# The delta rule's triangular inverse on 32x32 diagonal squares instead of whole 128x128 tiles

## Chip, core and metric

The kernel runs on one core of one Trainium2 chip. The metric is device time in microseconds (us), the median over runs; lower is better. One further execution was profiled, and its trace is what the views below are taken from.

## What is computed

Two layers of a hybrid trunk (a gated delta rule beside band attention, then a Mamba-2 mixer, each followed by a squared-ReLU MLP) on 256 positions of width 2048, all in f32. The edit touches one place of the first layer, the gated delta rule, with 8 heads of width 128. In the reference it works on chunks of 64 positions:

```python
lower = jnp.where(strict, jnp.einsum('bhnid,bhnjd->bhnij', kb, kc) * decay, 0.0)
eye = jnp.eye(CHUNK, dtype=f32)
tmat = lax.linalg.triangular_solve(eye + lower, jnp.broadcast_to(eye, lower.shape),
                                   left_side=True, lower=True, unit_diagonal=True)
u = jnp.einsum('bhnij,bhnje->bhnie', tmat, vc * bc[..., None])
w = jnp.einsum('bhnij,bhnjd->bhnid', tmat, kb * jnp.exp(gcum)[..., None])
```

`tmat` is the inverse of a unit lower triangular matrix. It then goes into every product with the values and the state. The kernel takes chunks of 128 positions, so it inverts a 128x128 matrix for each head and each of two chunks.

## The kernel before

The kernel is written for a scheduler: the Python code emits instructions through generators, and the framework places them on the five engines, in an order fixed at build time; on each engine instructions run in that order. The main thread emits weight blocks one after the other: a DMA brings 1 MB of weights (`raw`), ScalarE casts a half of them (`wh`, line 332), VectorE forms the rest (`wl`, line 336), and TensorE multiplies (line 322, the tiles `pg` and `pw`). After every few products a tick lets a step of the background generators in; each `yield` in such a generator ends a step. VectorE besides works off a stream of modulation rows, the `mraw` products of line 456.

The delta rule is such a background task, `gdn_group`, once for each of two head groups of four heads (`hg` 0 and 1); the second begins when the first is done. A group has two tiles, `gdn_tile` with `t` = 0 and 1, of 128 positions each, and steps them in turn. In a tile, `lt` (`gLt`) is the transposed strict lower triangle of four heads, 128x512, and the inverse is built by doubling: `x` (`gX`) holds the inverse of the diagonal blocks of size s, `xt` (`gXt`) its transpose. A level s takes, for each head, a product of `lt` and `x`, a mask and copy by VectorE into `y` (`gY`, cleared by GpSimd before), a product of `xt` and `y`, a subtraction by VectorE, and a transpose of `x` by TensorE that ScalarE copies into `xt`:

```python
for s in (2, 4, 8, 16, 32, 64):
    ...
    for h in range(4):
        self.mm(ps[:, h], lt[:, h], x[:, h])
    ...
    nc.vector.tensor_tensor(part(y, 0), part(ps, 0), self.M[s].unsqueeze(1).to_broadcast([P, 4, nb, s]), op=ALU.mult)
```

Level 64 makes the last update on `xt` itself and needs no transpose. The products `mm` (line 325) and transposes `tr` (line 329) of f32 tiles go to PSUM tiles `pm`, of which four buffers rotate. Beside the inverse the same stretch holds the attention of the same heads (`att_group`, score products `pm<-u,u`, transposes with `anti` and `aT`). When both tiles have an `x`, `gdn_group` sets the flag `prep`, which lets the attention of the first group start.

The masks of the levels (`lev2` to `lev64`, `lev1T`) are made by GpSimd at the start, in `masks`.

Of the kernel before, what the change touches and what calls it, by code (L numbers as in the profile page):

```python
# [12 lines left out]
I32 = mybir.dt.int32  # L13
AF = mybir.ActivationFunctionType
ALU = mybir.AluOpType
# [3 lines left out]
P = 128  # L19
# [93 lines left out]
class Trunk:  # L113
# [287 lines left out]
    def masks(self):  # L401
        nc = self.nc
        g = nc.gpsimd

        self.U = self.const([P, P], "Umask")
        g.memset(self.U, 1.0)
        g.affine_select(out=self.U, in_=self.U, compare_op=ALU.is_ge, fill=0.0, base=0, pattern=[[1, P]], channel_multiplier=-1)
        self.SU = self.const([P, P], "SUmask")
        g.memset(self.SU, 1.0)
        g.affine_select(out=self.SU, in_=self.SU, compare_op=ALU.is_ge, fill=0.0, base=-1, pattern=[[-1, P]], channel_multiplier=1)  # L410

        self.Uc = self.const([P, P], "Ucmask")
        g.tensor_copy(self.Uc, self.U)
        g.tensor_scalar(self.Uc[:64], self.Uc[:64], -1.0, None, op0=ALU.add)
        self.anti = self.const([P, P], "anti")
        g.memset(self.anti, 1.0)
        g.affine_select(out=self.anti, in_=self.anti, compare_op=ALU.is_equal, fill=0.0, base=1 - P, pattern=[[1, P]], channel_multiplier=1)

        self.M = {}
        for s in (2, 4, 8, 16, 32, 64):  # L420
            nb = P // (2 * s)
            m = self.const([P, nb, s], f"lev{s}")
            g.memset(m, 1.0)
            g.affine_select(out=m, in_=m, compare_op=ALU.is_ge, fill=0.0, base=-s, pattern=[[-2 * s, nb], [0, s]], channel_multiplier=1)
            g.affine_select(out=m, in_=m, compare_op=ALU.is_ge, fill=0.0, base=2 * s - 1, pattern=[[2 * s, nb], [0, s]], channel_multiplier=-1)
            self.M[s] = m

        self.M1T = self.const([P, 64, 2], "lev1T")
        g.memset(self.M1T, 0.0)
        v = self.M1T[:, :, 1:2]  # L430
        g.memset(v, 1.0)
        g.affine_select(out=v, in_=v, compare_op=ALU.is_equal, fill=0.0, base=0, pattern=[[-2, 64], [0, 1]], channel_multiplier=1)
        self.M1T = self.M1T.rearrange("p b c -> p (b c)")


    def mod_start(self, layer):
# [610 lines left out]
    def gdn_tile(self, hg, t, kf, qf, vf, G):  # L1047

        nc = self.nc
        H = slice(hg * 4, hg * 4 + 4)
        T = slice(t * P, t * P + P)
        v = self.small(8, "gss")
        for n, src in ((0, kf), (1, qf)):
            ps = self.pm()
            for h in range(4):
                self.tr(ps[:, h], src[:, h, T])
            if n == 0 and t == 0:
                kd = self.s2(tag="gkd")  # L1060
# [24 lines left out]
        nc.scalar.activation(E, ps, AF.Exp)  # L1085
        nc.vector.tensor_tensor(E, E, self.row(self.U), op=ALU.mult)
        yield
        ps = self.pm()
        for h in range(4):
            self.tr(ps[:, h], vf[:, h, T])  # L1090
        V = self.s2(tag="gV")
        nc.vector.tensor_tensor(V, ps, self.bc(nk), op=ALU.mult)
        G["V", t] = V
        yield

        ps = self.pm()
        for h in range(4):
            self.mm(ps[:, h], kf[:, h, T], kf[:, h, T])
        lt = self.s2(tag="gLt")
        for h in range(4):  # L1100
            nc.vector.scalar_tensor_tensor(lt[:, h], ps[:, h], be[:, h : h + 1], E[:, h], op0=ALU.mult, op1=ALU.mult)

        xt = self.s2(tag="gXt")
        nc.vector.tensor_tensor(xt, lt, self.row(self.M1T), op=ALU.mult)
        nc.vector.tensor_tensor(xt, self.row(self.ident), xt, op=ALU.subtract)
# [8 lines left out]
        ps = self.pm()  # L1114
        for h in range(4):
            self.tr(ps[:, h], xt[:, h])
        x = self.s2(tag="gX")
        nc.scalar.copy(x, ps)
        G["X" + str(t)] = x
        yield  # L1120


        for s in (2, 4, 8, 16, 32, 64):
            nb = P // (2 * s)
            part = lambda a, n: a.rearrange("p h (b n c) -> p h b n c", n=2, c=s)[:, :, :, n]
            ps = self.pm()
            for h in range(4):
                self.mm(ps[:, h], lt[:, h], x[:, h])
            y = self.s2(tag="gY")
            nc.gpsimd.memset(y, 0.0)  # L1130
            nc.vector.tensor_tensor(part(y, 0), part(ps, 0), self.M[s].unsqueeze(1).to_broadcast([P, 4, nb, s]), op=ALU.mult)
            yield
            ps = self.pm()
            if s < 64:
                for h in range(4):
                    self.mm(ps[:, h], xt[:, h], y[:, h])
                nc.vector.tensor_tensor(part(x, 0), part(x, 0), part(ps, 0), op=ALU.subtract)
                yield
                ps = self.pm()
                for h in range(4):  # L1140
                    self.tr(ps[:, h], x[:, h])
                nc.scalar.copy(xt, ps)
            else:
                for h in range(4):
                    self.mm(ps[:, h], y[:, h], xt[:, h])
                nc.vector.tensor_tensor(part(xt, 1), part(xt, 1), part(ps, 1), op=ALU.subtract)
                yield
        G["Xt", t] = xt

    def gdn_group(self, hg, kc, qc, vc, gates):  # L1150

        nc = self.nc
# [3 lines left out]
        G = {}  # L1156
        tiles = [Task(self.gdn_tile(hg, t, kf, qf, vf, G)) for t in range(2)]
        while not all(t.done for t in tiles):
            for t in tiles:
                if not t.done:  # L1160
                    t.step()
            if all("X" + str(n) in G for n in range(2)):
                self.prep[hg].done = True
            yield

        ps = self.pm()
        for h in range(4):
# [4 lines left out]
        ps = self.pm()  # L1172
# [5 lines left out]
        ps = self.pm()  # L1178
# [11 lines left out]
        ps = self.pm()  # L1190
# [6 lines left out]
        for t in range(2):  # L1197
            yield
            ps = self.pm()
# [24 lines left out]
        for t in range(2):  # L1224
            ps = self.pm()
# [608 lines left out]
```

## Time and profile before

| | |
|---|---|
| median of 3 runs | 2707.59 us (2705.99 to 2708.86) |
| the profiled execution | 2705.89 us, span 2704.0 us |
| TensorE's granted clock | 0.993 of full speed |
| HBM read | 675.33 MB |

The span is the time from the first to the last instruction of the profiled execution. "Busy" is the time in which an engine had at least one instruction under way. Matmuls overlap: one of 0.275 us can be followed by the next after 0.11 us, so the time that a row of them takes on TensorE is read from where the next begins. PE is TensorE's multiplication, PEld its loading of weights, DVE is VectorE, ACT ScalarE, POOL GpSimd. Rows of a timeline give start, length, engine, line, operation, the tiles written and read, and a count. Rows of groups give a count, then busy time and the mean of one in ns, then the idle time before them. Rows of a tile give the least, median and greatest duration in ns.

### The profile page before, as it was taken

To read this page: it belongs to the slowest core of one execution; us is meant where nothing else is said; L and a number is where in the kernel's file an instruction comes from. 1 tells how busy PE (TensorE), PEld (TensorE's weight loads), DVE (VectorE), ACT (ScalarE), POOL (GpSimd) and SP (SyncE) were. 2 spreads that over 40 slices of the span, in tenths; PEclk is the share of its full clock that TensorE was granted. 3 is DMA by queue.
4 is the path that set the end of the run, shared out by engine and by line. 5 is a ranking of instruction groups with operands and counts; after the bars stand their busy time and mean duration, and the time that the engine had idled before them with its cause. 6 is when DMAs were issued, how large, how long until landed. Compare 5 with 4: busy or idle time off the path is not lost.

```text
span 2704.0 us, 39515 instructions
## 1 busy us (share of the span) xinstructions
PE 2646.9 (98%) x15578; PEld 2337.1 (86%) x15578; DVE 2155.6 (80%) x3106; ACT 1348.6 (50%) x1990; POOL 24.2 (1%) x98
## 2 busy tenths in 40 slices
PE   5999999999999999999999999999999999999999
PEld 4887989888888888888888888888888888888888
DVE  7998998998888888889889876996787855555554
ACT  3444555455355354454556544655555354454452
POOL 1000000000000000000000000000000000000000
PEclk7999999999999999999999999999999999999999
DMA  9986487867899889988556665555557855555553
GB/s 350 354 326 235 169 313 266 317 248 284 315 348 329 334 326 334 331 326 300 181 182 212 224 234 203 203 179 180 196 187 290 323 201 190 187 187 187 188 193 133
DMA packets 100457, 680.05 MB, mean 251 GB/s; under 512 B 11184, under 2 KB 14512, under 8 KB 19376
## 3 DMA queue, kind: packets, MB, share of 16 engines
q1 hardware_dynamic: 95376, 669.07, 68.2%
q10 hardware_dynamic: 4896, 8.46, 1.1%
q8 instruction: 122, 2.00, 0.3%
q14 instruction: 63, 0.52, 0.1%
HBM read 675.33 MB, written 2.16 MB: 251 GB/s over the span
## 4 chain that ended last, share of the span: by engine, by line
PE 87%; DVE 7%; DMA 3%; ACT 2%; issue 1%; SPq 0%; ACTq 0%; DVEq 0%
PE pw L322 66%; PE pg L322 13%; PE pm L325 4%; PE pm L322 2%; DVE mraw L456 2%; DVE wl L336 2%; DMA mraw<-in_mod_dram 2%; PE pm L329 1%; DMA raw<-in_wo_ab_dram 1%; ACT wh L332 0%; DVE u L1614 0%; DVE hf L883 0%; DMA raw<-in_w_ab_dram 0%; DVE x L948 0%; ACT pm L1065 0%
## 5 line engine op out<-in xcount | busy, mean ns | idle before, releaser
L336 DVE TENSOR_TENSOR wl<-raw,wh 128x1024 fp32r<-128x1024 f32 x870 | 1051.0, 1220 | 440.0 <-ACT wh L332 437.3
L332 ACT CAST wh<-raw 128x1024 fp32r<-128x1024 f32 x870 | 905.6, 1051 | 991.4 <-PE pw L322 690.1
L322 PE MATMUL pw<-u,wh 128*128 128x512 f32 x5584 | 1321.2, 391 | 2.9 <-DVE x L948 1.5
L322 PEld LDWEIGHTS pw<-u,wh 128*128 128x128 f32 x5584 | 1031.7, 188 | 208.7 <-DVE x L948 1.5
L322 PEld LDWEIGHTS pw<-u,wl 128*128 128x128 f32 x5584 | 702.4, 191 | 22.7 <-issue 1.6
L322 PE MATMUL pw<-u,wl 128*128 128x256 f32 x5584 | 713.8, 283 | 1.5 <-DVE wl L336 0.7
L456 DVE SCALAR_TENSOR_TENSOR mraw<-mraw,crow 128x2048 f32<-128x2048 f32 x192 | 438.1, 2283 | 12.8 <-DMA mraw<-in_mod_dram 12.8
L322 PE MATMUL pg<-wh,u 128*128 128x512 f32 x864 | 281.8, 397 | 0.0
L322 PEld LDWEIGHTS pg<-wh,u 128*128 128x128 f32 x864 | 162.1, 188 | 32.3 <-issue 0.5
L948 DVE SCALAR_TENSOR_TENSOR x<-pw,mod,x 128x256 f32<-128x256 f32 x352 | 161.3, 478 | 32.7 <-PE pw L322 30.2
L322 PE MATMUL pg<-wl,u 128*128 128x512 f32 x432 | 169.6, 393 | 0.3
L322 PE MATMUL pg<-u,wh 128*128 128x256 f32 x672 | 124.5, 285 | 0.0
L322 PEld LDWEIGHTS pg<-u,wh 128*128 128x128 f32 x672 | 105.5, 192 | 0.3
L322 PEld LDWEIGHTS pg<-wl,u 128*128 128x128 f32 x432 | 81.3, 188 | 17.2 <-DVE wl L336 1.7
L322 PE MATMUL pg<-u,wl 128*128 128x256 f32 x336 | 95.5, 284 | 0.0
L322 PE MATMUL pm<-u,wh 128*128 128x256 f32 (+1 forms) x340 | 63.5, 291 | 19.2 <-ACT wh L332 19.2
L322 PEld LDWEIGHTS pm<-u,wh 128*128 128x128 f32 x340 | 53.9, 198 | 20.3 <-ACT wh L332 20.0
L322 PEld LDWEIGHTS pg<-u,wl 128*128 128x128 f32 x336 | 64.4, 192 | 0.0
L1007 DVE SCALAR_TENSOR_TENSOR u<-pad,cst,u 128x256 f32<-128x256 f32 x144 | 60.2, 477 | 4.4 <-ACT u L1001 4.3
L885 ACT ACTIVATE u<-hf,mod 128x256 fp32r<-128x256 f32 x64 | 29.3, 502 | 50.6 <-DVE hf L883 50.6
L1520 ACT COPY rs<-pw 128x512 f32<-128x512 f32 x64 | 36.9, 577 | 34.5 <-PE pw L322 34.5
L1526 ACT ACTIVATE rl<-rs 128x512 f32<-128x512 f32 x64 | 40.5, 633 | 23.7 <-DVE rs L1521 21.0
(298 smaller groups left out, 1556.0 us busy)
## 6 DMA issues: line engine op xcount, KB each, us to landing
raw<-in_w_dram SPq DMA_DIRECT2D x256, 1024.0 KB, 5.1
mraw<-in_mod_dram SPq DMA_DIRECT2D x192, 1024.0 KB, 6.2
raw<-in_w_ab_dram SPq DMA_DIRECT2D x56, 1024.0 KB, 5.4
raw<-in_w_ssd_dram SPq DMA_DIRECT2D x48, 1024.0 KB, 4.9
raw<-in_w_sz_dram SPq DMA_DIRECT2D x32, 1024.0 KB, 4.9
raw<-in_wo_ssd_dram SPq DMA_DIRECT2D x32, 1024.0 KB, 4.9
raw<-in_wo_ab_dram SPq DMA_DIRECT2D x16, 1024.0 KB, 7.0
sE<-sd_rowd ACTq DMA_DIRECT2D x32, 256.0 KB, 4.5
```

The costliest lines, as they stand in the source:

```text
L322: return self.nc.tensor.matmul(o, a, b, start=start, stop=stop, skip_group_check=True)
L325: self.nc.tensor.matmul(o, lhsT, rhs, start=True, stop=True, skip_group_check=True)
L329: return self.nc.tensor.transpose(o, a, self.anti if flip else self.ident[:k, :k])
L332: a = self.nc.scalar.copy(hi, src)
L336: b = self.nc.vector.tensor_tensor(lo, src, hi.bitcast(F32), op=ALU.subtract)
L456: x = nc.vector.scalar_tensor_tensor(raw, raw, 1.0, self.crow, op0=ALU.mult, op1=ALU.mult, accum_out=t[:, f : f + 1])
L885: nc.scalar.activation(hi, h[:, f], AF.Identity, bias=shift[:, col])
L948: self.last = nc.vector.scalar_tensor_tensor(x[:, 2 * b + f], ps[:, f, n], g[:, 2 * cb + f : 2 * cb + f + 1], x[:, 2 * b + f], op0=ALU.mul ...
L1007: nc.vector.scalar_tensor_tensor(h, pad[:, f, 1 + q : 257 + q], w[:, q, j : j + 1], h, op0=ALU.mult, op1=ALU.add)
L1520: nc.scalar.copy(lo, ps[:, :, 1])
L1526: nc.scalar.activation(rl, lo, AF.Relu)
```

## The change

The inverse leaves `gdn_tile`, which now ends with `lt` and the score tile `gPt`. A new generator `gdn_inverse` handles both tiles of a head group at once, after both are done. It keeps only the four 32x32 diagonal squares of each of the 8 matrices, in tiles of 128 partitions by 8 x 32: square b of all matrices lies on partitions 32b to 32b+31. Levels 2 to 16 stay within the squares: each product is 32x32x32, 32 of them to a step, in the four corners (b, b) of the array one after the other. VectorE transposes 32x32 blocks in place of TensorE. Two squares are then joined to a 64-block by 16 and 24 products of 32x32, and two 64-blocks to the whole by 8 and 8 products of 64x64. `XT` (`gXT`) is the full transposed inverse, cleared by GpSimd, and `x64` (`gX6`) the upper 64-block. ScalarE makes the copies of the joins.

```diff
@@ masks
+        def diagonal(name, full):
+            m = self.const([P, 32], name)
+            for b in range(4):
+                B = slice(32 * b, 32 * b + 32)
+                g.tensor_copy(m[B], full[B, B])
+            return m
+
+        self.I32 = diagonal("I32", self.ident)
         self.M = {}
-        for s in (2, 4, 8, 16, 32, 64):
+        for s in (2, 4, 8, 16):
...
@@ gdn_tile
-        xt = self.s2(tag="gXt")
-        nc.vector.tensor_tensor(xt, lt, self.row(self.M1T), op=ALU.mult)
-        nc.vector.tensor_tensor(xt, self.row(self.ident), xt, op=ALU.subtract)
+        G["lt", t] = lt
...
@@ new
+    def gdn_inverse(self, G):
...
+        for t in range(2):
+            for b in B:
+                nc.vector.tensor_tensor(xt[b, sub[t]], lt[t][b, :, b], rep(self.M1T[b], 4), op=ALU.mult)
+        nc.vector.tensor_tensor(xt, rep(self.I32, 8), xt, op=ALU.subtract)
+        nc.vector.transpose(flat(x), flat(xt))
...
+        for s in (2, 4, 8, 16):
+            ps = psum()
+            for n, t, h in heads:
+                for b in B:
+                    self.mm(ps[b, n], lt[t][b, h, b], x[b, n])
+            y = tile("gY")
+            nc.vector.tensor_tensor(y, ps, rep(self.M[s], 8), op=ALU.mult)
+            yield
+            ps = psum()
+            for n, t, h in heads:
+                for b in B:
+                    self.mm(ps[b, n], xt[b, n], y[b, n])
+            nc.vector.tensor_tensor(x, x, ps, op=ALU.subtract)
+            if s < 16:
+                nc.vector.transpose(flat(xt), flat(x))
             else:
+                for t in range(2):
+                    for b in B:
+                        nc.vector.transpose(XT[t][b, :, b], x[b, sub[t]])
+            yield
+
+        ps = psum()
+        for n, t, h in heads:
+            for p in (0, 2):
+                self.mm(ps[B[p + 1], n], lt[t][B[p], h, B[p + 1]], x[B[p], n])
+        y = tile("gY")
+        for p in (0, 2):
+            nc.scalar.copy(y[B[p + 1]], ps[B[p + 1]])
...
+        for n, t, h in heads:
+            self.mm(ps[B[1], n], XT[t][B[1], h, B[1]], y[B[1], n])
+            for p in (0, 2):
+                self.mm(ps[B[p], n], y[B[p + 1], n], XT[t][B[p + 1], h, B[p + 1]])
...
+        for n, t, h in heads:
+            self.mm(ps[upper, n], lt[t][lower, h, upper], x64[lower, n])
...
+        for n, t, h in heads:
+            self.mm(ps[lower, n], y[upper, n], XT[t][upper, h, upper])
...
@@ gdn_group
-            if all("X" + str(n) in G for n in range(2)):
-                self.prep[hg].done = True
-            yield
+            yield
+        self.prep[hg].done = True
+        yield from self.gdn_inverse(G)
```

How this moves instructions is seen in the built order of each engine. Below, a row gives line, operation, tiles (numbers tell buffers apart), the size written and a count. First TensorE at level 2 of the first head group, before:

```order
L325 MATMUL pm_2573<-gX_2546,gLt_2495 128x128 x4
L325 MATMUL pm_2581<-gX_2553,gLt_2508 128x128 x4
L325 MATMUL pm_2600<-u_2534,u_2338 128x128
L325 MATMUL pm_2600<-u_2534,u_2338 128x256
L325 MATMUL pm_2627<-gY_2578,gXt_2500 128x128 x4
L325 MATMUL pm_2633<-gY_2586,gXt_2513 128x128 x4
L322 MATMUL pg_2702<-hw_1725,raw_2557 128x256 x3
```

Each product comes twice, for tile 0 and tile 1, with attention scores (`u,u`) in between. The same place after:

```order
L325 MATMUL pm_2608<-gX_2577,gLt_2521 32x32 x16
L325 MATMUL pm_2608<-gX_2577,gLt_2531 32x32 x16
L325 MATMUL pm_2655<-u_2554,u_2364 128x128
L325 MATMUL pm_2655<-u_2554,u_2364 128x256
L322 MATMUL pg_2740<-hw_1751,raw_2563 128x256
L325 MATMUL pm_2670<-gY_2641,gXt_2576 32x32 x32
L322 MATMUL pg_2740<-hw_1751,raw_2563 128x256 x2
```

32 small products stand where 8 large ones did, and one more weight product has moved between the two halves of the level. Next TensorE in the second head group, at levels 8 and 16 before:

```order
L325 MATMUL pm_3754<-gY_3737,gXt_3540 128x128 x4
L329 MATMUL pm_3767<-ident,gX_3587 128x128 x4
L325 MATMUL pm_3773<-gX_3587,gLt_3522 128x128 x4
L329 MATMUL pm_3781<-ident,gX_3594 128x128 x4
L325 MATMUL pm_3787<-gX_3594,gLt_3535 128x128 x4
L325 MATMUL pm_3815<-gY_3778,gXt_3527 128x128 x4
L322 MATMUL pg_3808<-wh_4034,u_1713 128x512
```

The tiles take turns, so that one's products stand where the other waits for VectorE. After, from level 4 to the first join:

```order
L322 MATMUL pg_4037<-wh_4322,u_1739 128x512
L325 MATMUL pm_3862<-gX_3741,gLt_3679 32x32 x16
L325 MATMUL pm_3862<-gX_3741,gLt_3689 32x32 x16
L325 MATMUL pm_3904<-gY_3895,gXt_3740 32x32 x32
L325 MATMUL pm_3947<-gX_3741,gLt_3679 32x32 x16
L325 MATMUL pm_3947<-gX_3741,gLt_3689 32x32 x16
L325 MATMUL pm_3989<-gY_3980,gXt_3740 32x32 x32
L325 MATMUL pm_4044<-gX_3741,gLt_3679 32x32 x16
L325 MATMUL pm_4044<-gX_3741,gLt_3689 32x32 x16
L325 MATMUL pm_4094<-gY_4077,gXt_3740 32x32 x32
L325 MATMUL pm_4149<-gX_3741,gLt_3679 32x32 x8
L325 MATMUL pm_4149<-gX_3741,gLt_3689 32x32 x8
```

No other work stands between the products of three levels and the join's first. VectorE at the same levels, before:

```order
L1137 TENSOR_TENSOR gX_3587<-gX_3587,pm_3748 128x32x8
L336 TENSOR_TENSOR wl_4123<-raw_4120,wh_4122 128x1024
L1137 TENSOR_TENSOR gX_3594<-gX_3594,pm_3754 128x32x8
L1270 TENSOR_SCALAR ass_3835<-ass_3835 128x8
L336 TENSOR_TENSOR wl_4127<-raw_4120,wh_4126 128x1024
L1131 TENSOR_TENSOR gY_3778<-pm_3773,lev_260 128x16x16
```

and after:

```order
L1161 TENSOR_TENSOR gX_3741<-gX_3741,pm_3904 128x256
L467 SCALAR_TENSOR_TENSOR mraw_4478,mod_126<-mraw_4478,crow 128x2048
L1163 STREAM_TRANSPOSE gXt_3740<-gX_3741 128x256
L1155 TENSOR_TENSOR gY_3980<-pm_3947,lev_278 128x256
L336 TENSOR_TENSOR wl_4483<-raw_4480,wh_4482 128x1024
L336 TENSOR_TENSOR wl_4487<-raw_4480,wh_4486 128x1024
L1161 TENSOR_TENSOR gX_3741<-gX_3741,pm_3989 128x256
L467 SCALAR_TENSOR_TENSOR mraw_4543,mod_126<-mraw_4543,crow 128x2048
```

One mask and one subtraction of 256 elements serve both tiles, a transpose follows each subtraction, and the `wl` and `mraw` operations stand between them. GpSimd's order gains the small mask copies at the start and loses the clearing of `gY`; in SP's queue of DMAs the attention bias of the second head group now stands behind the next load of modulation rows, where it stood ahead of it.

More of the change, by code (lines that the diff above doesn't have):

```diff
@@ L417, in masks @@
         g.affine_select(out=self.anti, in_=self.anti, compare_op=ALU.is_equal, fill=0.0, base=1 - P, pattern=[[1, P]], channel_multiplier=1)
+        def diagonal(name, full):
[5 more added lines that the diff above has]
+        self.I32 = diagonal("I32", self.ident)
         self.M = {}
-        for s in (2, 4, 8, 16, 32, 64):
+        for s in (2, 4, 8, 16):
+            full = self.s2([P, P], tag="lev")
+            v = full.rearrange("p (b n c) -> p b n c", n=2, c=s)[:, :, 0]
             nb = P // (2 * s)
[L422 to L430, printed above, removed]
+            g.memset(full, 0.0)
+            g.memset(v, 1.0)
+            g.affine_select(out=v, in_=v, compare_op=ALU.is_ge, fill=0.0, base=-s, pattern=[[-2 * s, nb], [0, s]], channel_multiplier=1)
+            g.affine_select(out=v, in_=v, compare_op=ALU.is_ge, fill=0.0, base=2 * s - 1, pattern=[[2 * s, nb], [0, s]], channel_multiplier=-1)
+            self.M[s] = diagonal(f"lev{s}", full)
+        full = self.s2([P, P], tag="lev")
+        v = full.rearrange("p (b c) -> p b c", c=2)[:, :, 1:2]
+        g.memset(full, 0.0)
         g.memset(v, 1.0)
         g.affine_select(out=v, in_=v, compare_op=ALU.is_equal, fill=0.0, base=0, pattern=[[-2, 64], [0, 1]], channel_multiplier=1)
-        self.M1T = self.M1T.rearrange("p b c -> p (b c)")
+        self.M1T = diagonal("lev1T", full)
     def mod_start(self, layer):
@@ L1113, in gdn_tile @@
         yield
[L1114 to L1119, printed above, removed]
-        yield
[L1123 to L1131, printed above, removed]
-            yield
[L1133 to L1137, printed above, removed]
-                yield
[L1139 to L1142, printed above, removed]
-            else:
[L1144 to L1147, printed above, removed]
@@ L1148, in gdn_tile @@
-        G["Xt", t] = xt
+    def gdn_inverse(self, G):
+        nc = self.nc
+        lt = [G["lt", t] for t in range(2)]
+        heads = [(4 * t + h, t, h) for t in range(2) for h in range(4)]
+        B = [slice(32 * b, 32 * b + 32) for b in range(4)]
+        sub = [slice(4 * t, 4 * t + 4) for t in range(2)]
+        tile = lambda tag: self.s2([P, 8, 32], tag=tag)
+        flat = lambda a: a.rearrange("p n c -> p (n c)")
+        psum = lambda: self.pm([P, 512])[:, :256].rearrange("p (n c) -> p n c", c=32)
+        rep = lambda m, n: m.unsqueeze(1).to_broadcast([m.shape[0], n, 32])
+        xt, x = tile("gXt"), tile("gX")
+        for t in range(2):
[3 more added lines that the diff above has]
+        nc.vector.transpose(flat(x), flat(xt))
+        XT = [self.s2(tag="gXT") for _ in range(2)]
+        x64 = self.s2([P, 8, 64], tag="gX6")
+        for z in XT:
+            nc.gpsimd.memset(z, 0.0)
+        nc.gpsimd.memset(x64[B[0], :, 32:], 0.0)
+        yield
+        for s in (2, 4, 8, 16):
[5 more added lines that the diff above has]
+            nc.vector.tensor_tensor(y, ps, rep(self.M[s], 8), op=ALU.mult)
+            yield
+            ps = psum()
[5 more added lines that the diff above has]
+                nc.vector.transpose(flat(xt), flat(x))
+            else:
+                for t in range(2):
[9 more added lines that the diff above has]
+            nc.scalar.copy(y[B[p + 1]], ps[B[p + 1]])
+        nc.gpsimd.tensor_copy(x64[B[0], :, :32], x[B[0]])
+        nc.gpsimd.tensor_copy(x64[B[1], :, 32:], x[B[1]])
+        yield
+        ps = psum()
+        for n, t, h in heads:
+            self.mm(ps[B[1], n], XT[t][B[1], h, B[1]], y[B[1], n])
+            for p in (0, 2):
+                self.mm(ps[B[p], n], y[B[p + 1], n], XT[t][B[p + 1], h, B[p + 1]])
+        nc.vector.tensor_scalar(x64[B[1], :, :32], ps[B[1]], -1.0, None, op0=ALU.mult)
+        for t in range(2):
+            for p in (0, 2):
+                nc.scalar.activation(XT[t][B[p], :, B[p + 1]], ps[B[p], sub[t]], AF.Copy, scale=-1.0)
+        yield
+        lower, upper = slice(0, 64), slice(64, P)
+        ps = self.pm([P, 8, 64])
+        for n, t, h in heads:
+            self.mm(ps[upper, n], lt[t][lower, h, upper], x64[lower, n])
+        y = self.s2([P, 8, 64], tag="gY")
+        nc.scalar.copy(y[upper], ps[upper])
+        yield
+        ps = self.pm([P, 8, 64])
+        for n, t, h in heads:
+            self.mm(ps[lower, n], y[upper, n], XT[t][upper, h, upper])
+        for t in range(2):
+            nc.vector.tensor_scalar(XT[t][lower, :, upper], ps[lower, sub[t]], -1.0, None, op0=ALU.mult)
+            G["Xt", t] = XT[t]
+        yield
```

## Prediction, made before the changed kernel ran

> **What bounds the kernel now.** First the page's busy shares and chain, then a window over the stretch in which the edited code runs, then the edited tiles, then single steps.
>
> ```profile
> span 2704.0 us, 39515 instructions
> PE 2646.9 (98%) x15578; PEld 2337.1 (86%) x15578; DVE 2155.6 (80%) x3106; ACT 1348.6 (50%) x1990; POOL 24.2 (1%) x98
> PE 87%; DVE 7%; DMA 3%; ACT 2%; issue 1%; SPq 0%; ACTq 0%; DVEq 0%
> ```
>
> TensorE is the bound: 98% busy, 87% of the chain that ended last. So what counts is TensorE's own time in the inverse and any new wait of it. The stretch from 262 to 440 us holds the whole inverse of both head groups:
>
> ```profile
> core 0: us, PE busy (x) PEld busy (x) DVE busy (x) ACT busy (x) POOL busy (x), PEclk, DMA share, GB/s
> 262.00:440.00 178.00, 176.40 (x1193) 158.80 (x1192) 168.09 (x366) 89.83 (x224) 12.74 (x31) 1.00 0.69 255
> ```
>
> TensorE idles 1.6 us of 178 at full clock, but VectorE is busy too, 168.1 us (94%): TensorE cannot get much faster here before VectorE stops it.
>
> ```profile
> L325 PE MATMUL pm<-gX,gLt x192: 271/275/275, 273.9 to 420.8; 128*128 128x128 f32 x192
> L329 PE MATMUL pm<-ident,gX x80: 270/272/302, 279.5 to 419.9; 128*128 128x128 f32 x80
> L325 PE MATMUL pm<-gY,gXt x160: 270/275/275, 276.3 to 417.4; 128*128 128x128 f32 x160
> L325 PE MATMUL pm<-gXt,gY x32: 273/275/275, 317.3 to 424.8; 128*128 128x128 f32 x32
> L329 PE MATMUL pm<-ident,gXt x16: 270/272/300, 270.3 to 387.1; 128*128 128x128 f32 x16
> 270.33 0.60 PE L329 MATMUL pm<-ident,gXt 128*128 128x128 f32 x4
> 273.86 1.95 PE L325 MATMUL pm<-gX,gLt 128*128 128x128 f32 x16
> ```
>
> The inverse has 192+160+32 = 384 product steps and 80+16 = 96 transposes. 384 is twice the products of the code (96 in each of four tiles): an f32 product is two steps, a transpose one. The 275 ns are latency; steps overlap. Sixteen take 1.95 us, so one every (1.95-0.275)/15 = 0.112 us; transposes (0.60-0.272)/3 = 0.109. TensorE gives the inverse 384 x 0.112 + 96 x 0.109 = 53.5 us.
>
> **The change, part by part.** *Removed on TensorE:* these 53.5 us. *Added:* for each of two head groups 256 products of 32x32 in the levels and 16+24 in the first join, then 16 of 64x64. At two steps each that is 1184 small steps and 64 of 64x64. Two and a half times as many steps as before, so all hangs on what a 32x32 step costs. No row has it; these are near:
>
> ```profile
> L322 PEld LDWEIGHTS pg<-u,wn 128*32 128x32 f32 x16 | 1.7, 108 | 0.3
> L322 PEld LDWEIGHTS pg<-u,wn 128*64 128x64 f32 x16 | 2.1, 134 | 0.0
> L322 PEld LDWEIGHTS pg<-u,wn 128*128 128x128 f32 x16 | 3.0, 188 | 0.0
> 574.77 0.53 PEld L322 LDWEIGHTS pm<-ones,ss 128*128 128x128 f32 x4
> 575.22 0.30 PEld L322 LDWEIGHTS pm<-u,wl 128*128 128x128 f32 x2
> L322 PE MATMUL pg<-hw,raw 128*128 128x256 f32 x96 | 22.0, 379 | 0.0
> 227.68 7.03 PE L322 MATMUL pg<-raw,hw 128*128 128x512 f32 x16
> 233.69 1.02 PE L322 MATMUL pg<-raw,hw 128*128 128x512 f32 x2
> 234.64 0.24 PE L329 MATMUL pm<-ident,nb 32*128 32x32 f32 x1
> 234.72 0.22 PE L329 MATMUL pm<-ident,nb 32*128 32x32 f32 x1
> 234.87 0.70 PE L322 MATMUL pg<-raw,hw 128*128 128x512 f32 x1
> ```
>
> A weight load grows by (188-108)/96 = 0.83 ns a column. Products that move one single column (tile ones) still load every (575.22-574.77)/4 = 0.1125 us: 128 columns (0.106) plus some 0.006. So 32 columns load in 0.033 us. Moving 256 f32 columns takes 22.0/96 = 0.229 us a step, 32 of them 0.029. The low bound of a step in one place of the array is thus 0.033 us. The only pair of steps on 32 partitions with 32 columns moved (tile nb) stands 0.08 us apart, with 128 weight columns to load. I take 0.045, nearer to the low end because the load of 32 columns is the smaller one here, and keep both ends. 64x64: 64 x 0.83 ns + 0.006 = 0.059. Added: 1184 x 0.045 + 64 x 0.059 = 57.1 us; net of the 53.5, +3.6.
>
> [...]
>
> *Switching the array's tiling.* The nb pair is the one row where it goes from 128 to 32 rows and back. The stream before it steps by (7.03-0.59)/15 = 0.43 (0.59 = 1.02-0.43); after 233.69 and 234.12 the pair was due at 234.55 and came at 234.64, 0.09 late. The second step was over some 0.08 after 234.72 and the next stream came at 234.87, 0.07 late. One excursion costs about 0.16 us; the built order has 24 separate stretches of small products: +3.9 us. If small columns switch for free, 0.
>
> *New waits.* Before, two tiles ran in turn and each hid the other's VectorE step. Now both are in one tile: a product, VectorE, the next product.
>
> ```profile
> 281.48 1.06 PE L325 MATMUL pm<-gX,gLt 128*128 128x128 f32 x8
> 282.65 0.42 DVE L1131 TENSOR_TENSOR gY<-pm,lev 128x256 f32<-128x256 f32 x1
> 263.83 0.69 DVE L1092 TENSOR_TENSOR gV<-pm,gnk 128x512 f32<-128x512 f32 x1
> 264.57 1.16 PE L325 MATMUL pm<-u,u 128*128 128x128 f32 x8 [0.19 <-DVE gV L1092]
> ```
>
> One hand-over: the last step's latency 0.275 (less for its own slot), VectorE starts 282.65-282.54 = 0.11 later, works 0.42 on 128x256, and TensorE starts 264.57-264.52 = 0.05 after it: 0.8 us. In the order of the second head group (shown above) seven hand-overs have nothing, or 0.5 us, between them: levels 4, 8, 16 and into the first join. 7 x 0.8 = 5.6. In the first head group score products, weight blocks and transposes stand in the gaps; at 0.11 to 0.23 us a step they cover 0.7 to 3 us each, so I put 2 us for the few that are short. Sum +7.6; 0 if all is hidden, and the DVE rows below give the upper end.
>
> ```profile
> L456 DVE SCALAR_TENSOR_TENSOR mraw<-mraw,crow 128x2048 f32<-128x2048 f32 x26 | 59.2, 2281 | 1.5 <-DMA mraw<-in_mod_dram 1.5
> L336 DVE TENSOR_TENSOR wl<-raw,wh 128x1024 fp32r<-128x1024 f32 x32 | 38.9, 1217 | 3.0 <-ACT wh L332 3.0
> L1131 DVE TENSOR_TENSOR gY<-pm,lev 128x256 f32<-128x256 f32 x24 | 9.7, 416 | 0.7 <-PE pm L325 0.6
> L1137 DVE TENSOR_TENSOR gX<-gX,pm 128x256 f32<-128x256 f32 x20 | 8.1, 411 | 0.2
> L1104 DVE TENSOR_TENSOR gXt<-gLt,lev1T 128x512 f32<-128x512 f32 x4 | 2.7, 683 | 0.0
> L1105 DVE TENSOR_TENSOR gXt<-ident,gXt 128x512 f32<-128x512 f32 x4 | 2.7, 677 | 0.0
> L1146 DVE TENSOR_TENSOR gXt<-gXt,pm 128x256 f32<-128x256 f32 x4 | 1.6, 414 | 0.0
> L1313 DVE TENSOR_TENSOR as<-pm,u 128x128 f32<-128x128 f32 x4 | 1.1, 286 | 0.0
> ```
>
> *VectorE* loses 9.7+8.1+2.7+2.7+1.6 = 24.8 us. It gains per head group 8 masks of 128 elements and 8 small transposes (by size 0.28 each), 12 operations of 256 with the three transposes that replace TensorE's (0.41 each) and three of the joins: (16 x 0.28 + 15 x 0.41) x 2 = 21 us. No row shows a transpose on VectorE; between 0.28 and 0.48 for 256 elements it changes the sum by under 2 us. Net -3 to -4 us, which is off TensorE's path unless TensorE falls below VectorE.
>
> *ScalarE, GpSimd and SP's queue.*
>
> ```profile
> L1142 ACT COPY gXt<-pm x20: 565/586/592, 280.5 to 420.3; 128x512 f32<-128x512 f32 x20
> 193.20 0.10 POOL L964 MEMSET pad<- 128x6 f32 x1 [184.42 <-ACT wh L332]
> 419.40 0.39 SPq L1299 DMA_DIRECT2D u<-in_attn_rel_bias_dram  x1
> 425.45 0.33 SPq L453 DMA_DIRECT2D mraw<-in_mod_dram  x1
> 449.49 0.62 DVE L1313 TENSOR_TENSOR as<-pm,u 128x128 f32<-128x128 f32 x2 [1.70 <-issue]
> ```
>
> 20 copies of 0.586 us leave ScalarE, about seven smaller ones per group come; it has half its time free. GpSimd drops 24 memsets and gains two tiles to clear and two copies per group, and the masks' 24 small copies at the start. GpSimd waits 184 us ahead of 193.20, so even at 1 us each the copies are hidden. One DMA moves: the second group's attention bias stands behind the next mraw load, so it would go out at 425.45 at the earliest in place of 419.40; its first reader runs at 449.49, so 6 us stay covered, and beyond 30 us of delay VectorE would wait, and TensorE for it. All at nothing.
>
> **Sum:** 3.6 + 3.9 + 7.6 = +15 us. On the profiled execution's own 2705.9 us that is 2721; it was 1.7 us below the median of the runs, 2707.6, so the median is to be 2723.
>
> **The rivals.**
> *The step is 0.033 us, gain eaten by waits.* 39.1 + 3.8 = 42.9 us, 10.6 less than before. The switches give 3.9 back. In the second group VectorE now sets the pace: between the level-2 subtraction and the last transposes it has four mraw (9.1), four wl (4.9), seven masks and subtractions (2.9) and transposes of 1.2 + 2.2, 20.3 us, against TensorE's 1.8 + 6 x 64 x 0.033 + 1.1 = 15.6: 5 us of waits, and 3 in the first group. +1: 2709, no change.
> *The corners run side by side* (faster). Neighbouring products sit on other rows and columns of the array; if four overlap fully a step is 0.033/4 = 0.008 us, 1184 x 0.008 + 3.8 = 13 us, 40 less. But in this window VectorE has 178 - 168.1 + 3 = 13 us to spare, so no more than that can be won, less the hand-overs in which both stand: -9, 2699. It decides from a step under some 0.02 us on. [...] Against it: each step brings its own weights, and nothing in this trace loads faster than one after the other.
> *A floor per step* of 0.08 us, as in the nb pair: 94.7 + 3.8 = 98.5 us, +45, with switches and waits +56: 2764. For it: that pair. Against it: it loads four times the columns.
> The change could also shift which tile is late downstream; the products with V after it stand in the same place among the weight blocks, so I give that nothing.
>
> **How the numbers follow.** Step of 0.036 to 0.055 us (2712 to 2735): 0.45. Step near 0.033 with waits: 0.22. Side by side: 0.15. Floor of 0.06 or more: 0.18. A measurement can tell 0.2%, 5.4 us. Faster: most of the third case and a little of the second, 0.18. Same: the rest of the second and the low edge of the first, 0.24. Slower: 0.58. The range goes from the third case's 2698 into the lower half of the fourth, 2752.
>
> **What would show it.** Right: some 1250 matmul rows of 32x32 and 64x64 about 0.045 us apart; waits of PE on DVE gY and gX of 0.5 to 1 us in the second head group; PE busy still near 98%. Wrong: bursts of 64 steps in under 1.5 us (side by side) or over 4 us (floor); VectorE's transposes far from 0.4 us; waits of TensorE in the first group too.

## The result, and the profile after

The changed kernel is a little slower: 2715.16 us median of 6 runs (2713.45 to 2717.61), against 2706.93 us (2704.61 to 2708.86) for the kernel before in the same session, a ratio of 1.003 with a 95% interval of 1.002 to 1.004, or +8.2 us. The profiled execution took 2717.61 us.

From the page of the changed kernel, the span, the busy shares and the chain that ended last; then the window of the inverse, with the columns of the window shown before:

```profile
span 2715.9 us, 41012 instructions
PE 2630.3 (97%) x16346; PEld 2311.9 (85%) x16346; DVE 2155.5 (79%) x3114; ACT 1340.6 (49%) x1980; POOL 27.1 (1%) x106
PE 89%; DVE 8%; ACT 1%; DMA 1%; issue 1%; SPq 0%; ACTq 0%; DVEq 0%
```

```profile
262.00:440.00 178.00, 148.60 (x1873) 122.07 (x1872) 160.57 (x352) 74.92 (x194) 4.10 (x15) 0.88 0.65 244
```

In that window TensorE was busy 176.4 of 178 us before and is busy 148.6 now, at a granted clock of 0.88 in place of 1.00. It has much less to do there, and yet the kernel is later. The timeline of TensorE in the second head group's levels shows both sides (some rows between are left out, here and in the timelines below):

```profile
402.23 0.62 PE L322 MATMUL pg<-wh,u 128*128 128x512 f32 x2
402.78 0.75 PE L325 MATMUL pm<-gY,gXt 32*32 32x32 f32 x64
403.46 0.50 PE L322 MATMUL pg<-wl,u 128*128 128x512 f32 x1
405.50 0.40 PE L325 MATMUL pm<-gX,gLt 32*32 32x32 f32 x25
406.59 0.54 PE L325 MATMUL pm<-gX,gLt 32*32 32x32 f32 x39 [0.68 <-issue]
408.14 0.75 PE L325 MATMUL pm<-gY,gXt 32*32 32x32 f32 x64 [1.01 <-DVE gY L1155]
410.73 0.58 PE L325 MATMUL pm<-gX,gLt 32*32 32x32 f32 x25 [1.84 <-DVE gX L1161]
```

A set of 64 small steps takes 0.75 us, 0.19 of it the latency of the last: they start (0.75-0.191)/63 = 0.0089 us apart (0.191 us is the row of the tile below). (The expectations below take 7 to 8 ns for it.) 1184 x 0.0089 us, and the 64 steps of 64x64 at the 0.058 us that I find between their starts in the trace, make 14.2 us for what took 53.5: TensorE got 39 us back. What it lost again stands in the waits of TensorE from 262 to 460 us (total, times, longest):

```profile
PE pg L322 <- ACT wh L332: 8.5, 1, 8.5
PE pg L322 <- DVE wl L336: 5.6, 3, 3.4
PE pm L325 <- DVE gX L1161: 5.6, 4, 1.8
PE pm L325 <- DVE gY L1155: 4.6, 5, 1.2
PE pm L325 <- issue: 1.6, 3, 0.7
```

Half of it is at weight products, not in the inverse. These rows of TensorE, around the end of the first group and the start of the second, show such waits and what follows them:

```profile
351.16 0.80 PE L322 MATMUL pg<-wl,u 128*128 128x512 f32 x1 [3.39 <-DVE wl L336]
351.75 1.06 PE L322 MATMUL pg<-wh,u 128*128 128x512 f32 x2
355.12 0.62 PE L322 MATMUL pg<-wh,u 128*128 128x512 f32 x2
360.48 0.39 PE L322 MATMUL pg<-wh,u 128*128 128x512 f32 x1
369.37 0.79 PE L322 MATMUL pg<-wh,u 128*128 128x512 f32 x1 [8.50 <-ACT wh L332]
371.42 1.05 PE L322 MATMUL pg<-wh,u 128*128 128x512 f32 x2
375.16 0.63 PE L322 MATMUL pg<-wh,u 128*128 128x512 f32 x2
```

Behind each gap a pair of steps takes 1.06 or 1.05 us in place of 0.62, for some 3 to 5 us: the granted clock is 0.50 from 351.2 to 354.3 us and from 369.4 to 374.8, and 1.00 behind both. The wait of 3.39 us ends with a `wl`. That is what remains of the loaded weights when their rounded copy `wh` is taken off, so it needs the load, then ScalarE's cast, then VectorE. VectorE's timeline at that place without its small operations, after and then before, and the cast:

```profile
341.21 2.28 DVE L467 SCALAR_TENSOR_TENSOR mraw<-mraw,crow 128x2048 f32<-128x2048 f32 x1
343.50 2.28 DVE L467 SCALAR_TENSOR_TENSOR mraw<-mraw,crow 128x2048 f32<-128x2048 f32 x1
345.79 2.28 DVE L467 SCALAR_TENSOR_TENSOR mraw<-mraw,crow 128x2048 f32<-128x2048 f32 x1
349.89 1.22 DVE L336 TENSOR_TENSOR wl<-raw,wh 128x1024 fp32r<-128x1024 f32 x1
```

```profile
339.30 2.28 DVE L456 SCALAR_TENSOR_TENSOR mraw<-mraw,crow 128x2048 f32<-128x2048 f32 x1
341.59 1.22 DVE L336 TENSOR_TENSOR wl<-raw,wh 128x1024 fp32r<-128x1024 f32 x1
343.01 2.28 DVE L456 SCALAR_TENSOR_TENSOR mraw<-mraw,crow 128x2048 f32<-128x2048 f32 x1
345.30 1.22 DVE L336 TENSOR_TENSOR wl<-raw,wh 128x1024 fp32r<-128x1024 f32 x1
```

```profile
346.17 1.05 ACT L332 CAST wh<-raw 128x1024 fp32r<-128x1024 f32 x1 [4.30 <-DMA raw<-in_w_ab_dram]
```

Before, modulation rows and `wl` alternate. Now three rows come in a row, 6.9 us. Only the last of them stands in the way of this `wl`, for the weights themselves were late: their load went out at 341.31, after 2.7 us in which SP's queue waited for an earlier `wl` of VectorE, and the cast was done at 347.22. From there to 349.89 VectorE's queue held the `wl` back, 0.8 us by the third row and 1.9 us by a chain of small operations (348.00 to 349.89). So some 2.7 of the 3.39 us are VectorE's order of work. The 8.50 us follow from it. The load of those weights had gone out at 348.10. ScalarE's queue holds the copies `u` of TensorE's transposes, then 20 squares (360.24 to 366.8 us) with eight operations `gu` (to 368.26), and only then the next casts of weights; the transposes came at 357.17, behind the late weights. ScalarE's wait for them from 340 to 380 us was 8.6 us, against 2.2 before:

```profile
ACT u L1284 <- PE pm L329: 8.6, 1, 8.6
```

### The profile page after: what moved, and what is told of

Read it like the earlier page. It is cut to its first block, busy times and chain, and to the rows that moved or that the text cites. A ratio compares the mean times of both kernels' runs of the same rounds, so it can differ in the third digit from the quotient of the medians.

```text
span 2715.9 us, 41012 instructions
## 1 busy us (share of the span) xinstructions
PE 2630.3 (97%) x16346; PEld 2311.9 (85%) x16346; DVE 2155.5 (79%) x3114; ACT 1340.6 (49%) x1980; POOL 27.1 (1%) x106
## 4 chain that ended last, share of the span: by engine, by line
PE 89%; DVE 8%; ACT 1%; DMA 1%; issue 1%; SPq 0%; ACTq 0%; DVEq 0%
PE pw L322 70%; PE pg L322 13%; PE pm L325 3%; DVE mraw L467 2%; PE pm L322 2%; DVE wl L336 2%; PE pm L329 1%; DVE u L1670 0%; ACT wh L332 0%; ACT pm L1076 0%; DVE hf L894 0%; DMA raw<-in_w_ab_dram 0%; DVE u L897 0%; DVE u L993 0%; DMA sE<-sd_rowd 0%
## 5 line engine op out<-in xcount | busy, mean ns | idle before, releaser
L1577 DVE TENSOR_TENSOR rs<-pw,rs 128x512 f32<-128x512 f32 x64 | 43.8, 684 | 10.0 <-ACT rs L1576 10.0
```

Of the source, the lines that this page charges most:

```text
L1577: nc.vector.tensor_tensor(lo, ps[:, :, 0], lo, op=ALU.add)
```

## The experiments

Three theories stood against each other. A: TensorE's work did fall by some 40 us, and VectorE's load in that stretch keeps the kernel from using it. B: the small steps are not what A takes them for, in the two forms that their runs state. C: the chain product, VectorE, product is itself the loss. A2 came to it later: the half clock costs the time. Ratios are to the kernel before, run in the same session.

**What a small step costs: corner and triple.** In the first, the four corners are not taken in turn:

```diff
-            for n, t, h in heads:
-                for b in B:
+            for b in B:
+                for n, t, h in heads:
```

> The changed kernel, with the level products of a step sorted by corner: 16 products in corner 0, then 16 in corner 1 and so on, instead of the four corners in turn. Nothing is left out. In the changed kernel's trace the small steps start 7 ns apart. Theory A (neighbouring products run side by side because they lie in different corners): within one corner the steps stand 0.03 to 0.05 us apart, the 1024 level steps take 30 to 50 us of TensorE in place of some 8, and the kernel is slower than the changed one by 5 to 30 us, the rest being covered by waits that are there already. Rival B (any two small steps follow each other at 7 ns, whatever their corner): the distances and the time stay as they are, within 4 us.

Measured: 2728.18 us, 1.0077 (1.0061 to 1.0094), some 13 us above the changed kernel. TensorE's timeline of this run has sets of 64 of two lengths:

```profile
414.32 1.91 PE L325 MATMUL pm<-gX,gLt 32*32 32x32 f32 x64
419.35 3.06 PE L325 MATMUL pm<-gX,gLt 32*32 32x32 f32 x64 [0.69 <-DVE gX L1161]
```

(1.91-0.191)/63 = 0.027 us a step in one corner, three times the 0.0089 of corners in turn; the granted clock is 0.98 from 400 to 420 us, where the first row lies, and 0.50 from 420 to 440, into which the second reaches. The order of the corners is all that differs between the two kernels, so the speed comes from neighbouring products lying in different corners, as A has it. 1024 x 0.018 = 19 us more of TensorE's time cost 13: the rest fell into the waits on gX and gY, which went from 10.2 to 3.4 us.

In the second, every set is issued three times:

```diff
-            for n, t, h in heads:
+            for n, t, h in heads * 3:
```

> The changed kernel with each level product on the small squares issued three times into the same place (2048 more small steps, the result is the same). Theory A (a small step costs TensorE 7 to 8 ns): 15 us more of TensorE, partly inside waits that are there anyway, so 0 to 15 us slower than the changed kernel. Rival B' (a step really costs some 0.045 us, as I had predicted, and the close starts in the records are only issue times): 92 us more, of which at most 27 us fit into the waits: 60 us slower or more.

Measured: 2760.79 us, 1.0198 (1.0183 to 1.0213), 45 us above the changed kernel, between both expectations. TensorE's timeline, its waits from 262 to 500 us, and the row of the instruction queue over the whole span (packets, MB), here and in the changed kernel:

```profile
425.13 0.44 PE L325 MATMUL pm<-gX,gLt 32*32 32x32 f32 x28
428.14 1.93 PE L325 MATMUL pm<-gX,gLt 32*32 32x32 f32 x128 [2.57 <-issue]
432.42 0.74 PE L325 MATMUL pm<-gX,gLt 32*32 32x32 f32 x36 [2.34 <-issue]
436.42 1.61 PE L325 MATMUL pm<-gY,gXt 32*32 32x32 f32 x103 [0.32 <-issue]
```

```profile
PE pm L325 <- issue: 30.6, 15, 4.5
```

```profile
q8 instruction: 144, 2.36, 0.3%
```

```profile
q8 instruction: 128, 2.10, 0.3%
```

The steps are hardly dearer: 128 of them in 1.93 us, in a window (420 to 440 us) whose granted clock is 0.67. But TensorE stands and waits for nothing that the profile shows, 15 times, for 2.0 us in the mean and up to 4.5. In these rows 128 products, which are 256 instructions with their weight loads, lie from one such wait to the next. The period counts other products too: between the waits that end at 432.42 and at 436.42 lie 36 small steps, 3 weight products and 89 small steps, 128 together. A backlog of small steps that are dearer than they look would not count the weight products. In the changed kernel's own trace such waits end at 406.59, 411.69 and 417.33 us, with 128 products from one to the next. 16 packets (0.26 MB, 16 KB each) were added on the instruction queue for 4096 instructions, 256 to a packet by division. I read this as TensorE running through the small steps faster than their instructions arrive: 30.6 us of such waits here, 1.6 in the changed kernel. 2048 x 0.0089 = 18 us of steps and 29 us more of these waits would make 47. That the measured 45 lies so near is in part chance, for the waits on wh, wl, gX and gY fell by 13 us meanwhile, while the clock was low for longer (0.50 from 440 to 460 us). The price of a step is settled against the prediction's 0.045; that the waits are the instruction supply is read from the period and the packets, and was not tried otherwise.

**VectorE's load: light_before and light_after.** The same edit in both kernels leaves out 1792 of the 2048 elements of 48 rows, and nothing of their loads:

```diff
-    x = nc.vector.scalar_tensor_tensor(raw, raw, 1.0, self.crow, op0=ALU.mult, op1=ALU.mult, accum_out=t[:, f : f + 1])
+    c = 256 if layer == 0 and v in (2, 3, 4) else 2048
+    x = nc.vector.scalar_tensor_tensor(raw[:, :c], raw[:, :c], 1.0, self.crow[:, :c], op0=ALU.mult, op1=ALU.mult, accum_out=t[:, f : f + 1])
```

> The kernel before with the same cut of the 48 modulation rows (256 of 2048 elements, the rest of these dot products left out). TensorE was 98% busy in it from 262 us on, so by all theories it gains little: 0 to 8 us, at 2699 to 2707. A gain of 15 us or more would say that VectorE held the kernel before too.

> The changed kernel with VectorE's modulation rows of the first layer's rows 2, 3 and 4 (48 rows, worked off between about 200 and 600 us) taken over 256 of their 2048 elements: these dot products are left incomplete, each takes some 0.4 us instead of 2.28, and VectorE loses about 90 us of work there. The loads are unchanged. Theory A (the inverse gives TensorE 41 us back, and VectorE's load in that stretch keeps the kernel from using them): this kernel ends 15 to 40 us before the kernel before with the same cut, at about 2670 to 2690. Rival C (the loss is the chain of hand-overs itself, product, VectorE, product, and the switches of the array's tiling, which a lighter VectorE doesn't shorten): it ends 0 to 10 us behind the kernel before with the same cut.

Measured: 2707.22 us, 0.9996 (0.9987 to 1.0006), for before, which gains nothing, and 2693.90 us, 0.9951 (0.9936 to 0.9966), for after: 13.3 us faster than before with the same cut. The sign turns, as A expected and C didn't, if by a little less than A's 15. Windows of before, after, light_before and light_after, in this order:

```profile
262.00:460.00 198.00, 195.74 (x1348) 177.55 (x1347) 185.33 (x398) 99.90 (x243) 12.74 (x31) 1.00 0.69 253
```
```profile
262.00:460.00 198.00, 168.46 (x2037) 141.45 (x2036) 178.40 (x389) 85.54 (x219) 4.10 (x15) 0.90 0.64 241
```
```profile
262.00:460.00 198.00, 195.07 (x1334) 176.65 (x1333) 140.24 (x392) 97.96 (x238) 13.33 (x32) 1.00 0.69 252
```
```profile
262.00:460.00 198.00, 185.01 (x2217) 157.08 (x2217) 147.45 (x421) 97.55 (x247) 5.11 (x15) 0.97 0.67 256
```

With light rows TensorE idles 13 us instead of 29.5 and its clock is 0.97 instead of 0.90; without the change it is full either way. The same cut is thus worth nothing to the kernel before and 21 us to the changed one: the rows' work on VectorE takes a good part of the gain. The largest wait of TensorE that is left from 262 to 500 us in the changed kernel with light rows is none of VectorE's:

```profile
PE pm L325 <- issue: 7.1, 4, 3.3
```

It is of the kind seen in the triple run, a wait for nothing that the profile shows. With full rows TensorE waits for VectorE more often, and only 1.6 us of such waits are seen.

**Where the rows stand: spread and spread_before.** Nothing is left out; the rows get another pace:

```diff
-        self.rate, self.rate2 = 0.25, 1.1
+        self.rate, self.rate2 = 0.25, 0.6
...
-        self.rate = 0.5
+        self.rate = 0.6
         self.b_block(w, GZ, ...)
...
+        self.rate = 0.8
         self.out_blocks(i["wo_ab"], ...)
```

> The changed kernel with the pace of the modulation rows altered, nothing else: 0.6 in place of 1.1 rows' steps per tick while the second head group's inputs are made, then 0.6 in place of 0.5 and 0.8 in place of 0.5 up to the end of the layer's output product. The rows come later and evenly, and none is left out. Theory A (rows crowd VectorE there, and wait in the buffers that the weights' loads need too, so weights are late: TensorE's waits of 8.5 and 5.6 us on wh and wl): these two waits fall below 5 us together, and the kernel is 4 to 12 us faster than the changed one, near or below the kernel before. Rival (the waits come from the inverse's chain alone): within 3 us of the changed one.

> The kernel before with the same altered pace of the modulation rows. TensorE is full there, so by all theories the time stays within 4 us of the kernel before; a gain like that of the changed kernel with this pace would mean that the pace is worth it by itself, without the change.

Measured: 2723.13 us, 1.0063 (1.0047 to 1.0079), and 2738.89 us, 1.0118 (1.0102 to 1.0134): both slower, against both expectations, and the changed one again 15.8 us ahead of the other. The first residual addition, in a row of its line (first and last start), tells the two halves apart, for before, after and spread:

```profile
L948 DVE SCALAR_TENSOR_TENSOR x<-pw,mod,x x352: 462/477/486, 500.9 to 2700.5; 128x256 f32<-128x256 f32 x176
```
```profile
L959 DVE SCALAR_TENSOR_TENSOR x<-pw,mod,x x352: 468/478/488, 510.7 to 2712.3; 128x256 f32<-128x256 f32 x176
```
```profile
L959 DVE SCALAR_TENSOR_TENSOR x<-pw,mod,x x352: 472/479/492, 493.6 to 2718.9; 128x256 f32<-128x256 f32 x176
```

The changed kernel loses its time ahead of this point: it comes 9.8 us later than before, and the last addition 11.8 us later. In the spread run the stretch of the inverse ended 17 us sooner than in the changed kernel, and TensorE's waits on wh and wl in it were gone. Then the rows that had moved met the layer's output product, where TensorE waited for VectorE's `wl`, 17.0 us in the changed kernel with this pace (the row below) and 17.9 in the kernel before with it:

```profile
PE pw L322 <- DVE wl L336: 17.0, 7, 6.1
```

So A held for the stretch, and I had overlooked that VectorE is as full behind it (38.8 of 40 us from 500 to 540 in the kernel before). That the rows' place decides where TensorE waits is shown. Whether they do it by VectorE's time alone or also by the load buffers was not separated: in the kernel's code rows and weights share the four buffers `raw`.

**The clock and the chain: fill and two.** The first puts eight unused 128x128 steps behind each set of the second group:

```diff
...
+                for h in range(4):
+                    self.mm(fill[0], lt[0][:, h], lt[1][:, h])
...
```

> The changed kernel, with eight extra 128x128 f32 steps on TensorE (0.9 us, their result is not used) behind each of the eight sets of level products of the second head group, where TensorE waited 0.9 to 1.8 us for VectorE. Nothing else changes. Theory A2 (the idle time in these hand-overs halves the granted clock, 0.73 and 0.76 in the windows 400 to 440 us, and part of the loss comes from that): the clock there goes back to 0.9 or more and the kernel is 2 to 6 us faster than the changed one, for the extra steps lie inside the waits. Rival (the half clock costs nothing, since VectorE sets the pace there): no change, or up to 5 us slower, where an extra step delays the next set.

Measured: 2718.62 us, 1.0045 (1.0029 to 1.0061). The window from 400 to 420 us, changed kernel first:

```profile
400.00:420.00 20.00, 11.86 (x529) 9.29 (x527) 19.71 (x27) 8.27 (x22) 0.00 (x0) 0.73 0.95 363
```
```profile
400.00:420.00 20.00, 15.79 (x455) 12.72 (x453) 19.57 (x26) 7.57 (x18) 0.00 (x0) 1.00 0.99 376
```

The clock is back at 1.00 there and nothing is won: A2's gain of 2 to 6 us did not come, in a place in which VectorE is busy 19.6 of 20 us. The added steps are 7 us of TensorE's own work (an estimate: 64 at the 0.11 us of a 128x128 step in the kernel before), so a small gain by the clock may be hidden in what they cost. For the gaps at 351 and 369 us it wasn't tried.

The second gives each tile its own chain, the two stepped in turn, with twice as many VectorE operations of half the size:

```diff
-        yield from self.gdn_inverse(G)
+        inv = [Task(self.gdn_inverse(G, t)) for t in range(2)]
+        while not all(t.done for t in inv):
+            for t in inv:
+                if not t.done:
+                    t.step()
+            yield
...
```

> The changed kernel with the small-square inverse done for each of the two tiles by itself, the two stepped in turn, as the tiles were before; the same products in sets of 16 in place of 32, twice as many VectorE operations of half the size, some 4 us more VectorE in all. Rival C (the hand-overs cost: with both tiles in one chain nothing stands between a product and the VectorE step that it waits for): the waits on gX and gY, 10.2 us in the changed kernel, fall to some 3, and the kernel is 5 to 10 us faster than the changed one. Theory A (VectorE's load keeps TensorE waiting, whatever the order): 0 to 6 us slower than the changed one.

Measured: 2716.25 us, 1.0034 (1.0019 to 1.0049), as the changed kernel, though its five runs lie far apart (2710.86 to 2719.71) and the profiled one, 2711.26, near their low end. Of the 10.2 us on gX and gY one wait on gX remains that counts:

```profile
PE pm L325 <- DVE gX L1137: 4.7, 3, 4.1
```

Half of those waits went, and the first residual addition still comes at 510.7 us, as in the changed kernel; others came in their place, 4.6 us on the attention's `as` and 3.3 on `gu` among them. So at the old pace the chain alone isn't the loss.

**A milder pace: pace and pace_before, pace_pool, pace_two.** The pace is 0.85 in place of 1.1, 0.8 in the two gate blocks, and 0.5 as before in the output product:

```diff
-        self.rate, self.rate2 = 0.25, 1.1
+        self.rate, self.rate2 = 0.25, 0.85
...
-        self.rate = 0.5
+        self.rate = 0.8
         self.b_block(w, GZ, ...)
...
+        self.rate = 0.5
         self.out_blocks(i["wo_ab"], ...)
```

> The changed kernel with another pace of the modulation rows, a milder one than in the spread run: 0.85 in place of 1.1 while the second head group's inputs are made, 0.8 in place of 0.5 during the two gate blocks behind it, and the old 0.5 in the layer's output product, where the spread run had lost some 25 us. About three rows of 2.28 us are thereby taken out of the stretch in which TensorE waits and put where VectorE has idle time; behind the gate blocks one or two more come than in the changed kernel. Theory A (VectorE's load at the wrong place eats the gain): the first residual addition, at 511 us in the changed kernel and 494 in the spread one, comes at 497 to 505, the output product is not slowed, and the time is 2700 to 2710, 5 to 15 us below the changed kernel. Rival (total VectorE work up to the layer's end decides, wherever it stands): 2713 to 2720, as the changed kernel.

> The kernel before with the pace of the pace run. TensorE is the bound there, and the rows behind the gate blocks are about as many as in the pace run: within 5 us of the kernel before by all theories. If the pace run is faster than this one, the change is worth something by itself once VectorE's rows are out of its way.

Measured: 2703.92 us (2700.20 to 2706.29, 11 runs), 0.9988 (0.9980 to 0.9997), and 2711.90 us (2709.12 to 2713.14, 11 runs), 1.0018 (1.0009 to 1.0027). With this pace the change is worth 8.0 us, and the time is in A's range, 11 us below the changed kernel. Against the kernel before at its own pace only 2.2 us are left: the milder pace costs that kernel 5.8 us, a little more than the 5 allowed for. The first residual addition comes 14 us sooner than in the changed kernel:

```profile
L959 DVE SCALAR_TENSOR_TENSOR x<-pw,mod,x x352: 469/478/486, 496.8 to 2697.5; 128x256 f32<-128x256 f32 x176
```

Two versions were to take more from it. In pace_pool GpSimd makes the inverse's first tile (`nc.gpsimd.tensor_tensor` in the two places of `nc.vector.tensor_tensor` ahead of the first transpose):

> The kernel of the pace run, in which besides GpSimd in place of VectorE makes the first small tile of the inverse (8 masks of 32x128 and one subtraction per head group). VectorE loses 18 operations, 2 x (8 x 0.28 + 0.41) = 5.3 us. GpSimd is idle for over 98% of the span, but each group's inverse begins later by what GpSimd needs more (its rows of 32x256 took 0.39 us, so some 4 us a group in place of 2.7). Theory A: 2 to 6 us faster than the pace run. Rival C (the chain's length decides): 0 to 4 us slower than it.

Measured: 2709.36 us, 1.0013 (1.0004 to 1.0021), 5.4 us slower than pace. GpSimd's masks of 32x128 took twice VectorE's 0.28 us:

```profile
L1139 POOL TENSOR_TENSOR gXt<-gLt,lev1T 32x128 f32<-32x128 f32 x16 | 9.1, 570 | 101.1 <-DVE gLt L1112 65.5 <-DVE at L276 34.8
```

8 x 0.57 and one of 1.16 make 5.7 us ahead of the first level in place of 2.7, in each group: less VectorE work, a later chain, a slower kernel, by more than the 4 us that C allowed. Here C's side showed.

> The two separate chains of the run two (each tile's inverse by itself, the two in turn) together with the pace of the pace run. In the run two the waits on gX and gY fell from 10.2 to 4.7 us and the time did not move, with VectorE at 93% or more in the windows around; with the rows out of the way that cover should now count. If VectorE's load and the uncovered hand-overs each cost something (theory A and rival C together): 2 to 6 us faster than the pace run, 2698 to 2702. If VectorE's load alone decides, its 4 us more of small operations show: 0 to 5 us slower than the pace run.

Measured: 2714.15 us, 1.0026 (1.0016 to 1.0036), 10 us slower than pace, against both expectations. The waits on gX and gY fell below 1 us, and another rose: the attention of the second group, `as`, now came late, from 262 to 640 us

```profile
PE pm L329 <- DVE as L1372: 8.7, 4, 3.8
```

with VectorE busy 38.8 of 40 us from 460 to 500 us, where three of these waits lie. Which of its operations pushed the scores back was not settled.

## Why the prediction was right, and where it was not

The direction came out and the size roughly: +15 us forecast, +8.2 measured. The way there did not: the terms were off by far, to opposite sides, and that their sum came near is luck.

- *Removed, 53.5 us:* holds as far as the busy time can tell: over the whole execution it fell by 16.6 us (2646.9 to 2630.3), and 39 us of steps less at a lower clock fit that.
- *Added, 57.1 us at 0.045 us a step:* this step of the prediction failed. The steps stand 0.0089 us apart, and the term is 14.2 us: -39 in place of +3.6. I took one product to load its weights behind the other; the corner run shows 0.027 us for that even in one corner, and corners in turn go three times as fast. The rival "corners side by side" had the step right (0.008) and its time wrong (2699). The prediction's own sign of it, 64 steps in under 1.5 us, is there: 0.75 us.
- *The floor per step,* 0.08 us as in the nb pair, is not there: starts are 8.9 ns apart in the mean, in one corner 27.
- *Switches, 3.9 us:* about as put. The set at 402.78 was due at 402.69 (0.62 less 0.39 to 402.46, and 0.23) and the next weight product came 0.12 us after the last small start (403.46 less 403.34): 0.2 us, by this one place, for each of 24 places, 5 us.
- *Hand-overs, 7.6 us:* 10.2 us on gX and gY. In the second group they are six waits of 1.0 to 1.8 us where seven of 0.8 were put, since VectorE's queue holds other operations between: its subtractions start at 404.72, 410.27 and 415.74, and in each of these 5.5 us stand a row of 2.28 and two `wl` of 2.33 together. Right in kind.
- *ScalarE, GpSimd and SP's queue, "all at nothing":* the second step that failed. I moved the inverse's own operations and one DMA, and did not ask what the modulation rows and the weight casts do when the inverse's rows on VectorE go elsewhere in its order: 8.5 + 5.6 us of waits for weights. The rival "step 0.033" came nearest here: it let VectorE set the pace, with 5 and 3 us of waits, where 24 came.
- *VectorE, -3 to -4 us:* the rows after are 4.8 + 4.5 + 3.3 + 3.2 + 2.6 us for the small transposes, masks, gX, gY and larger transposes, and some 4 us of single ones, 22.4 against the 24.8 removed; VectorE's busy time over the whole execution stayed (2155.6 and 2155.5 us). Its transposes of 256 elements took 0.436 us, near the 0.41 assumed; the second row is the source of the 0.191 us above:

```profile
L1163 DVE STREAM_TRANSPOSE gXt<-gX x6: 424/436/437, 279.6 to 418.3; 128x256 f32<-128x256 f32 x6
L325 PE MATMUL pm<-gY,gXt x512: 191/191/258, 276.3 to 419.9; 32*32 32x32 f32 x171
```

- *The clock* was in no term. 0.90 over 198 us (the window above) is some 20 us of full clock less, part of it in idle time. -39 for the steps, +27 for the idle time (29.5 less 2.3) and up to +20 for the clock make about +8, while the first residual addition came 10 us later. This is an estimate: idle time and low clock overlap, and the places where the tiling switches are not in it.
- *The rival's bound* was the useful sentence: "no more than that can be won" of VectorE's spare time. It was read as a gain of 9, but in this kernel VectorE, 94% busy, had no room to be reordered either.

So the sum came out near because a saving of 39 us that I had not seen was eaten by waits that I had put at 7.6 us and a low clock that I had not put at all. With lighter or better placed rows 8 to 16 of the 39 us come out. An estimate for the light rows, from their windows: 10 us more idle time (13.0 less 2.9), of which the waits for nothing that the profile shows are 7.1, up to 6 us of clock (0.03 of 198) and 5 of switches leave 18; the first residual addition comes 15.7 us sooner (487.4 against 503.1). Not separated stays what the early `prep` does, which the same edit sets ahead of the inverse, so that the first group's attention may start sooner.

## What to carry to other kernels

Before crediting time saved on the engine that is the bound, look how busy the next engine is in the same stretch and in the one behind it: here, with VectorE at 94%, a saving of 39 us ended in a loss of 8, and moving VectorE's other work by a pace setting turned it into a gain of 8 over the same setting without the change, and of 2 over the kernel before at its own setting. Such a change and the settings tuned around the old code are one thing and have to be tried together. Let small products change corner from one to the next: in these runs that was 8.9 ns a step, in one corner 27.

## What the hardware showed that I had not expected

- Small f32 steps in four corners in turn start 8.9 ns apart, in one corner 27 ns; steps of 64x64, 58 ns.
- TensorE stood between small products and waited for nothing that the profile shows: 15 times and 30.6 us in the triple run, up to 4.5 us at once, 7.1 us and up to 3.3 with light rows, 1.6 us in the changed kernel, there with 128 products from one wait to the next. 128 products and their 128 weight loads are gone in 1.1 us (128 x 0.0089), and the triple run's 4096 instructions more came with 16 packets more on the instruction queue. That TensorE outran its instructions is my reading of this.
- After a gap of 3.39 us TensorE ran at half clock (0.43 us a step in place of 0.23, granted clock 0.50) for some 3 us, after one of 8.5 us for 5.
